# Streaming encoder step: first weights on ScalarE's queue, one query panel in the opening, later key transposes and operand splits

## The chip, the cores and the metric

The program runs on one core of a Trainium2 chip. The time is device microseconds of one execution. The kernel before took 2278.07 us, the median of three runs (2276.33 to 2283.46).

## The reference

One step of a one-layer encoder works on 1024 new prompt frames and on 8 running streams of 16 frames, with model width 2048 and 8 heads of 128 for each of two head groups. All of it is float32.

```
h = rms_norm(x, norm_pre);  p = h @ w_in            # 2048 -> 8 x 1024: q,k,v,gate of both groups
o_sb = stick_breaking(q_sb, k_sb, v_sb)             # samples also over 1024 cached frames
o_r  = retention(rope(q_r), rope(k_r), v_r, state)  # per-head decay, chunks of 64
y = concat(head_norm(o_sb)*silu(gate_sb), head_norm(o_r)*silu(gate_r)) @ w_out
x + rms_norm(y, norm_post)     # and the new keys, values and states
```

## The kernel before

**Products.** Each float32 operand is split into a high and a low float32r half (ScalarE copies `wh<-wr`, VectorE subtracts `wl<-wr,wh`; lines 167 and 168), and each product is three matmuls: high by high, low by high, high by low. Tokens are in two groups: group 0 holds prompt tiles 0 to 3 and the samples (640 columns, in pieces of 256 and 384), group 1 prompt tiles 4 to 7 (512 columns). A *panel* is one head's 128 columns of one of the eight projections, `project(g, mov, col(c, h))`: c is 0 for the stick-breaking queries, 1 keys, 3 gate, 4 retention queries, 5 retention keys, 7 retention gate. A panel of group 0 is 16 x 3 x 2 = 96 matmuls, one of group 1 is 48. The weights of a panel come in four loads `wr` of 256 KB on SP's queue, through five buffers.

**Stages.** The *opening* (lines 511 to 614) makes the panels q and k of retention head 0 while x arrives, computes row sums of squares (`squares`, on ScalarE, from loads `xt`), turns them into reciprocal roots (`rows_of`, VectorE) and spreads these over the partitions with four small matmuls `pb<-dg,ones` (`spread`, line 557). Then come the eight heads of group 0, the eight heads of group 1, and the *output stage*, in which seven products in the manner of Strassen are formed of sums of blocks. Its left operands are loaded and split by `left` and `left_sample` (tiles `ah`/`al` from loads `yr`, `sh`/`sl` from loads `ys`, `mh`/`ml` from loads `mr`).

**What sets the order.** A head's other work is written as generators, wrapped in `Job`. After each step of a panel, `tick()` advances one clock and runs the next step of at most one job that is due; what a generator yields is the number of ticks to its next step. So the constants `D_...` set the place of that work among the products. `drain(job)` calls `tick()` until the job is done, without products in between. A scheduler then orders each engine's instructions by their place in the program and by when it thinks that their inputs are ready; `pin` adds that an instruction may not stand ahead of the last product written before it, and `tied` adds the same in group 0 alone (`phase[0] == 0`). On the chip every engine, and SP's queue too, goes through its list in order.

**Jobs that the change touches.** `ret_branch` (lines 1022 to 1040) does the retention of one head: it writes the rotated keys to memory (`s_rk`), loads them back with blocks exchanged (`ro<-s_rk`, on SP), waits `D_TI` ticks, transposes them on VectorE (`rkn<-ro`, line 1032) and scales them (line 1036) before TensorE's `pS<-rv,rkn` (line 946). `retention` also reads the samples' state (`st<-state`, TensorE `pa<-st,rq`, line 976). In the first head of group 0 it starts in `ret_start`. The stick-breaking job of a head ends, for the samples, with the decode: `kp<-be` is transposed, `pd<-vn,kp` and `pd<-vc,kp` (lines 878 and 886) multiply the cached values `vc` (512 KB loads on SP, line 849, six buffers, so each waits until TensorE has read an older one), and `do<-pd` is copied, normed (`sq`, `or`, `do<-do,or`) and written (`s_o<-do`, on ScalarE's queue).

Of the kernel before, what the change touches and what calls it, by code (L numbers as in the profile page):

```python
# [18 lines left out]
P = 128  # L19
# [7 lines left out]
NT = PT + 1  # L27
SAMPLE = PT
WQ = 4
D_X = (5, 4)  # L30
X_PIECES = ((0, 256), (256, 384), (640, 512))
KC_AHEAD = 2
COLS = (0, 1, 3, 4, 5, 7)
# [55 lines left out]
def tile_hybrid_step(  # L89
# [151 lines left out]
    def drain(job):  # L241
        while job is not None and not job.done:
            tick()
# [67 lines left out]
    def left(gi, n, hi, lo, bufs, tag, deep):  # L311
        src = LEFT[n]
        raw = []

        def load(h):
            r = bufs.tile([P, 256], F32, name=tag, tag=tag, bufs=deep)
            if src[0] == "y":
                pin(nc.sync.dma_start(r, s_y[gi][src[1] * H + h][:, src[2] * 256 : src[2] * 256 + 256]))
            else:
                pin(nc.sync.dma_start(r, s_s[gi][h][:, src[1], :]))  # L320
            raw.append(r)

        for h in range(deep - 1):
            load(h)
        yield D_OP
        for h in range(HT):
            if h + deep - 1 < HT:
                load(h + deep - 1)
            r = raw.pop(0)
            pin(*split(hi[h], lo[h], r))  # L330
            yield D_OP

    def left_sample(kk, hi, lo, bufs, tag, deep):
        raw = []

        def load(h):
            r = bufs.tile([P, P], F32, name=tag, tag=tag, bufs=deep)
            pin(nc.sync.dma_start(r, s_y[0][kk * H + h][:, 4 * P : 5 * P]))
            raw.append(r)

        for h in range(deep - 1):
            load(h)
        yield D_OP
        for h in range(HT):
            if h + deep - 1 < HT:
                load(h + deep - 1)
            pin(*split(hi[h], lo[h], raw.pop(0)))
            yield D_OP
# [20 lines left out]
        made = [pool.tile([P, HT, n], F32R, name=t, tag=t, **kw) for t in tags]  # L369
        return [[t[:, h] for h in range(HT)] for t in made]  # L370

    def load_w(col):
        hs, ls = [], []
        for w in range(KT // WQ):
            wr = wp.tile([P, WQ, P], F32, name="wr", tag="wr", bufs=5)
            nc.sync.dma_start(wr, w_cols[COLS.index(col[0]), col[1], :, w * WQ : (w + 1) * WQ, :])
            wh = wp.tile([P, WQ, P], F32R, name="wh", tag="wh")
            wl = wp.tile([P, WQ, P], F32R, name="wl", tag="wl")
            split(wh, wl, wr)
            yield w, wh, wl  # L380
# [20 lines left out]
    def project(g, mov, col):  # L401
        acc = acc_banks(g)
        for w, wh, wl in load_w(col):
            products(mov, acc, g["pieces"], w, wh, wl)
        return list(zip(acc, g["pieces"]))
# [57 lines left out]
    with ExitStack() as s1:  # L463
# [47 lines left out]
        with tc.tile_pool(name="p0", bufs=2) as p0, tc.tile_pool(name="p0s", bufs=1) as p0s, tc.tile_pool(  # L511
            name="p0p", bufs=4, space=PSUM
        ) as p0p:
            warm = p0s.tile([P, 1], F32, name="warm")
            nc.scalar.activation(warm, eps, AF.Sqrt)
            ones = p0s.tile([P, P], F32, name="ones")
            nc.vector.memset(ones, 1.0)
            nc.sync.dma_start(pre, pre_cols)
# [1 line left out]
            def load_cols(piece, k, m):  # L520
                o, n = X_PIECES[piece]
                xc = p0.tile([P, m, n], F32, name=f"xc{piece}", tag=f"xc{piece}", bufs=4)
                src = x_cols[:, KT * o : KT * (o + n)].rearrange("p (k n) -> p k n", k=KT)
                nc.sync.dma_start(xc, src[:, k : k + m, :])
                return xc

            def squares(tiles, ssq, pace):
                todo = [(i, t, c) for i, t in enumerate(tiles) for c in range(2)]
                raw = []

                def load(i, t, c):
                    xt = p0.tile([P, HALF], F32, name="xt", tag="xc0", bufs=4)
                    nc.sync.dma_start(xt, x_rows(t)[:, c * HALF : (c + 1) * HALF])
                    raw.append(xt)

                for item in todo[:4]:
                    load(*item)
                yield pace
                for n, (i, t, c) in enumerate(todo):
                    xt = raw.pop(0)  # L540
                    pin(nc.scalar.activation(xt, xt, AF.Square, accum_out=ssq[:, c, i : i + 1]))
                    if n + 4 < len(todo):
                        load(*todo[n + 4])
                    yield pace
# [14 lines left out]

            def second_panel(w):  # L560
                wr = wp.tile([P, WQ, P], F32, name="wr", tag="wr", bufs=5)
                nc.sync.dma_start(wr, w_cols[COLS.index(5), 0, :, w * WQ : (w + 1) * WQ, :])
                wh, wl = (p0s.tile([P, WQ, P], F32R, name=f"w{s}5{w}") for s in "hl")
                split(wh, wl, wr)
                return w, wh, wl

            tiles = g0["tiles"]
            accs = [acc_banks(g0), acc_banks(g0)]
            first_panel = load_w(col(4, 0))
            panels = [], []  # L570
            xcs = [], []
            for w in range(KT // WQ):
# [31 lines left out]

            ret_values(g0, mov, 0, None, roots_first)
            rooted_tables((*first, *ropes), X_PIECES[:2])
            job = Job(squares(GROUPS[1]["tiles"], ssq[1], D_X[1]))
            tick()
            first = *first, pair["r"][:, :, 0, :], dict(rg=gate(project(g0, mov, col(7, 0)), "rg"))
            drain(job)  # L610
            nc.vector.tensor_copy(root_of[:, len(tiles) :], rows_of(ssq[1], "p4"))
            rb = p0s.tile([P, NB_TOK], F32, name="rb4")
            spread(rb, root_of, len(tiles), last)
            nc.scalar.dma_start(s_root, rb)

        kq = s1.enter_context(tc.tile_pool(name="kq", bufs=1))
        zp = s1.enter_context(tc.tile_pool(name="zp", bufs=1))
# [404 lines left out]
        def ret_branch(gi, g, h, rq, rk, rv, rest):  # L1022
            nt = len(g["tiles"])
            rkn = ep.tile([P, 6, P], F32, name="rkn", tag="rkn")

            out = Out(nt, "ro")
            s = turn_out(rk[:, : nt * P].rearrange("p (k t) -> p k t", t=P), f"s_rk{gi}_{h}")
            yield D_TO[phase[0]]
            raw = out.o.rearrange("p k d -> p (k d)")
            turn_in(s, raw, nc.sync)  # L1030
            yield D_TI[phase[0]]
            tied(nc.vector.transpose(rkn.rearrange("p k d -> p (k d)")[:, : nt * P], raw))
            if SAMPLE in g["tiles"]:
                nc.vector.tensor_scalar(rkn[:, 5, :], rkn[:, 4, :], dec[:, h, 5:6], None, ALU.mult)
                nc.vector.tensor_scalar(rkn[:, 4, :], rkn[:, 4, :], dec[:, h, 4:5], None, ALU.mult)
            nc.vector.tensor_scalar(rkn[:, :4, :], rkn[:, :4, :], dec[:, h, 1:2], None, ALU.mult)
            yield from retention(gi, g, h, out, rq, rk, rkn, rv)
            while "rg" not in rest:
                yield 3
            yield from out.finish(1, h, rest["rg"], rk, s_y[gi][H + h])  # L1040
# [35 lines left out]
        for gi, g in enumerate(GROUPS):  # L1076
# [7 lines left out]
            for h in range(H):  # L1084
# [29 lines left out]

                def attention():
                    nonlocal sb_job, sub, ip
                    acc = project(g, mov, col(0, h))
                    held = project(g, mov, col(1, h)) if h == H - 1 else None
                    drain(sb_job)
                    if gi == 1 and h == 0:  # L1120
# [459 lines left out]
```

## Time and profile before

| what | value |
|---|---|
| time, median of 3 runs | 2278.07 us |
| the profiled execution's own time | 2280.05 us |
| its span | 2278.3 us |
| PE busy | 2241.5 us (98%) |
| DVE, ACT, POOL busy | 1263.7, 919.8, 340.6 us (55%, 40%, 15%) |
| mean granted clock of TensorE | 0.996 |
| moved by DMA | 463.13 MB, mean 203 GB/s |

How to read it: the execution took 1.75 us more than its span, and the span is what the trace shows. TensorE is busy in nearly all of it, so what a change of order can move is the idle time of TensorE and the matmuls that run slower just after such a pause. In the timeline the first column is the start, the second the time until the instruction's end; matmuls overlap, so the pace of matmuls is the distance of their starts, not their duration. A timeline row stands for several instructions when it ends in x and a count.

### The profile page before, as it was taken

To read this page: it belongs to the slowest core of one execution; us is meant where nothing else is said; L and a number is where in the kernel's file an instruction comes from. 1 tells how busy PE (TensorE), PEld (TensorE's weight loads), DVE (VectorE), ACT (ScalarE), POOL (GpSimd) and SP (SyncE) were. 2 spreads that over 40 slices of the span, in tenths; PEclk is the share of its full clock that TensorE was granted. 3 is DMA by queue.
4 is the path that set the end of the run, shared out by engine and by line. 5 is a ranking of instruction groups with operands and counts; after the bars stand their busy time and mean duration, and the time that the engine had idled before them with its cause. 6 is when DMAs were issued, how large, how long until landed. Compare 5 with 4: busy or idle time off the path is not lost.

```text
span 2278.3 us, 38962 instructions
## 1 busy us (share of the span) xinstructions
PE 2241.5 (98%) x14306; PEld 2023.3 (89%) x14306; DVE 1263.7 (55%) x2606; ACT 919.8 (40%) x1951; POOL 340.6 (15%) x577
## 2 busy tenths in 40 slices
PE   8999999999999999999999999999999999999998
PEld 8999999999999999999887989888888988788886
DVE  5435544454545454456556665766665667555567
ACT  6433333333333333335343334343343445435363
POOL 0012120301202030121111111120212212000020
PEclk9999999999999999999999999999999999999999
DMA  8747656675656657578778888878787758865596
GB/s 284 233 153 199 196 159 194 176 220 159 182 194 181 194 165 209 177 200 269 193 225 207 220 220 235 206 226 238 220 231 213 216 165 190 252 205 182 146 222 172
DMA packets 440832, 463.13 MB, mean 203 GB/s; under 512 B 182336, under 2 KB 302144, under 8 KB 440128
## 3 DMA queue, kind: packets, MB, share of 16 engines
q1 hardware_dynamic: 318400, 300.16, 46.5%
q0 software_dynamic: 28720, 78.41, 12.3%
q10 hardware_dynamic: 93520, 82.07, 11.4%
q8 instruction: 112, 1.84, 0.3%
q14 instruction: 80, 0.66, 0.1%
HBM read 359.58 MB, written 110.36 MB: 206 GB/s over the span
## 4 chain that ended last, share of the span: by engine, by line
PE 88%; DMA 5%; DVE 3%; issue 2%; ACT 2%; SPq 0%; POOL 0%; DVEq 0%; ACTq 0%; POOLq 0%
PE acc L387 46%; PE accn L446 17%; PE a L1213 5%; PE a L1214 5%; PE a L1210 5%; PE pa L783 3%; PE z L753 2%; PE pd L886 1%; PE zc L822 1%; DMA ro<-s_rk 1%; DMA s_rk<-rk 1%; PE pa L931 1%; PE pS L946 1%; DVE kp L682 1%; DMA wr<-w_cols 1%
## 5 line engine op out<-in xcount | busy, mean ns | idle before, releaser
L387 PE MATMUL acc<-mh,wh 128*128 128x256 f32 (+2 forms) x2304 | 667.4, 341 | 6.9 <-ACT wh L167 6.9
L387 PE MATMUL acc<-ml,wh 128*128 128x256 f32 (+2 forms) x2304 | 662.7, 340 | 0.2
L387 PE MATMUL acc<-mh,wl 128*128 128x256 f32 (+2 forms) x2304 | 659.8, 338 | 0.0
L168 DVE TENSOR_TENSOR wl<-wr,wh 128x512 fp32r<-128x512 f32 x504 | 345.9, 689 | 428.0 <-ACT wh L167 401.7
L167 ACT ACTIVATE wh<-wr 128x512 fp32r<-128x512 f32 x504 | 317.3, 631 | 641.2 <-PE acc L387 347.2
L387 PEld LDWEIGHTS acc<-mh,wh 128*128 128x128 f32 x2304 | 421.4, 189 | 39.2 <-ACT wh L167 6.9
L387 PEld LDWEIGHTS acc<-ml,wh 128*128 128x128 f32 x2304 | 422.9, 189 | 32.1 <-issue 3.3
L387 PEld LDWEIGHTS acc<-mh,wl 128*128 128x128 f32 x2304 | 425.5, 189 | 27.8 <-DVE wl L168 0.2
L446 PE MATMUL accn<-whn,mh 128*128 128x256 f32 x1152 | 328.1, 285 | 0.0
L446 PE MATMUL accn<-wln,mh 128*128 128x256 f32 x1152 | 325.8, 283 | 0.8 <-DVE wln L168 0.8
L446 PE MATMUL accn<-whn,ml 128*128 128x256 f32 x1152 | 325.7, 283 | 0.0
L446 PEld LDWEIGHTS accn<-whn,mh 128*128 128x128 f32 x1152 | 220.7, 192 | 2.7 <-issue 0.8
L446 PEld LDWEIGHTS accn<-wln,mh 128*128 128x128 f32 x1152 | 220.7, 192 | 1.8 <-DVE wln L168 1.0
L446 PEld LDWEIGHTS accn<-whn,ml 128*128 128x128 f32 x1152 | 220.7, 192 | 0.0
L167 ACT ACTIVATE whn<-wrn 128x512 fp32r<-128x512 f32 x128 | 80.5, 632 | 183.2 <-PE acc L387 74.2
L168 DVE TENSOR_TENSOR wln<-wrn,whn 128x512 fp32r<-128x512 f32 x128 | 87.6, 687 | 117.4 <-ACT whn L167 113.5
L646 POOL DMA_DIRECT2D be<-s_be x128 | 94.1, 741 | 149.5 <-DMA s_be<-be 126.4
L682 DVE TENSOR_TENSOR_SCAN kp<-kp 128x1152 f32<-128x1152 f32 (+4 forms) x40 | 82.7, 2067 | 45.7 <-POOL kp L671 29.1
L809 POOL DMA_DIRECT2D kcT<-cache_k x64 | 34.6, 545 | 442.2 <-PE pd L886 268.2
L1210 PE MATMUL a<-wh,mh 128*128 128x512 f32 x240 | 94.0, 392 | 1.8 <-ACT wh L167 1.8
L671 POOL TENSOR_SCALAR_AFFINE_SELECT kb<-kb 128x128 f32<-128x128 f32 x64 | 29.8, 474 | 433.2 <-ACT kb L665 430.9
L1213 PE MATMUL a<-wl,mh 128*128 128x512 f32 x240 | 94.3, 393 | 0.2 <-DVE wl L168 0.2
(272 smaller groups left out, 2968.7 us busy)
## 6 DMA issues: line engine op xcount, KB each, us to landing
wr<-w_cols SPq DMA_DIRECT2D x384, 256.0 KB, 4.4
wrn<-w_rows SPq DMA_DIRECT2D x128, 256.0 KB, 3.7
kcT<-cache_k POOLq DMA_DIRECT2D x64, 512.0 KB, 8.2
vc<-cache_v SPq DMA_DIRECT2D x64, 512.0 KB, 6.0
wr<-s_b SPq DMA_DIRECT2D x80, 256.0 KB, 4.1
br<-w_out SPq DMA_DIRECT2D x64, 256.0 KB, 4.9
s_b<-br ACTq DMA_DIRECT2D x32, 512.0 KB, 5.5
wr<-w_out SPq DMA_DIRECT2D x48, 256.0 KB, 3.7
```

What stands on the lines that cost most here:

```text
L167: nc.scalar.activation(hi, src, AF.Copy),
L168: nc.vector.tensor_tensor(lo, src, hi.bitcast(F32), ALU.subtract),
L387: last = nc.tensor.matmul(a[:, :m], lhs[:, j, :], rhs[w][:, j, o : o + m], start=(w == 0 and j == 0 and n == 0), stop=(w == KT // WQ - 1 a ...
L446: anchor[0] = nc.tensor.matmul(a, lhs[q][:, jj, ts], rhs[:, j, :], start=(w == 0 and j == 0 and n == 0 and t % 2 == 0), stop=(w == KT // 2 ...
L646: q.dma_start(raw[32 * i : 32 * i + 32, :].rearrange("p (k a) -> p k a", a=32), s[:, :, 32 * i : 32 * i + 32].rearrange("k (j b) a -> b (k ...
L682: nc.vector.tensor_tensor_scan(rev, rev, rev, 1.0, ALU.mult, ALU.bypass)
L753: nc.tensor.matmul(z[:, :c], q2[a][:, i * P : (i + 1) * P], k2[b][:, s : s + c], start=(m == 0), stop=(m == 2),)
L783: nc.tensor.matmul(po[:, :P], at[:, j, :], vn[:, j, :], start=(j == 0), stop=(j == t))
L809: ready.append((kc, nc.gpsimd.dma_start(kc, cache_k[h, m // 4, m % 4])))
L1210: ins = nc.tensor.matmul(a, hi[k][:, ts], wh, start=first, stop=False)
L1213: nc.tensor.matmul(a, hi[k][:, ts], wl, start=False, stop=False)
L1214: anchor[0] = nc.tensor.matmul(a, lo[k][:, ts], wh, start=False, stop=last)
```

## The change

Four edits, built into one program:

1. *Opening loads.* The first `wr` of both first panels are issued on ScalarE's queue, ahead of the table load and the warming activation, which move behind them. The first 512 KB load of x becomes four of 128 KB.
2. *First query panel.* The second group's roots become part of the job (`later_roots`), with the pace of its squares changed from 4 to 5 ticks, and the panel `project(g0, mov, col(0, 0))` is written ahead of `drain(job)`; the first attention uses that panel. `ret_start` thereby stands one panel (48 ticks) later in the program.
3. *Key transposes.* `D_RK = (32, 19)` takes the place of `D_TI = (32, 13)` in `ret_branch`: nothing changes in group 0, six ticks more in group 1.
4. *Operand splits.* `left` and `left_sample` wait `D_LAND` = 12 ticks after their first loads, not `D_OP` = 2.

```diff
--- before.py
+++ after.py
@@ -27,7 +27,9 @@
 NT = PT + 1
 SAMPLE = PT
 WQ = 4
-D_X = (5, 4)
+D_X = (5, 5)
+D_RK = (32, 19)
+D_LAND = 12
 X_PIECES = ((0, 256), (256, 384), (640, 512))
 KC_AHEAD = 2
 COLS = (0, 1, 3, 4, 5, 7)
@@ -322,7 +324,7 @@
 
         for h in range(deep - 1):
             load(h)
-        yield D_OP
+        yield D_LAND
         for h in range(HT):
             if h + deep - 1 < HT:
                 load(h + deep - 1)
@@ -340,7 +342,7 @@
 
         for h in range(deep - 1):
             load(h)
-        yield D_OP
+        yield D_LAND
         for h in range(HT):
             if h + deep - 1 < HT:
                 load(h + deep - 1)
@@ -369,11 +371,10 @@
         made = [pool.tile([P, HT, n], F32R, name=t, tag=t, **kw) for t in tags]
         return [[t[:, h] for h in range(HT)] for t in made]
 
-    def load_w(col):
-        hs, ls = [], []
+    def load_w(col, first=nc.sync):
         for w in range(KT // WQ):
             wr = wp.tile([P, WQ, P], F32, name="wr", tag="wr", bufs=5)
-            nc.sync.dma_start(wr, w_cols[COLS.index(col[0]), col[1], :, w * WQ : (w + 1) * WQ, :])
+            (nc.sync if w else first).dma_start(wr, w_cols[COLS.index(col[0]), col[1], :, w * WQ : (w + 1) * WQ, :])
             wh = wp.tile([P, WQ, P], F32R, name="wh", tag="wh")
             wl = wp.tile([P, WQ, P], F32R, name="wl", tag="wl")
             split(wh, wl, wr)
@@ -511,8 +512,6 @@
         with tc.tile_pool(name="p0", bufs=2) as p0, tc.tile_pool(name="p0s", bufs=1) as p0s, tc.tile_pool(
             name="p0p", bufs=4, space=PSUM
         ) as p0p:
-            warm = p0s.tile([P, 1], F32, name="warm")
-            nc.scalar.activation(warm, eps, AF.Sqrt)
             ones = p0s.tile([P, P], F32, name="ones")
             nc.vector.memset(ones, 1.0)
             nc.sync.dma_start(pre, pre_cols)
@@ -521,7 +520,9 @@
                 o, n = X_PIECES[piece]
                 xc = p0.tile([P, m, n], F32, name=f"xc{piece}", tag=f"xc{piece}", bufs=4)
                 src = x_cols[:, KT * o : KT * (o + n)].rearrange("p (k n) -> p k n", k=KT)
-                nc.sync.dma_start(xc, src[:, k : k + m, :])
+                step = 1 if piece == k == 0 else m
+                for j in range(0, m, step):
+                    nc.sync.dma_start(xc[:, j : j + step, :], src[:, k + j : k + j + step, :])
                 return xc
 
             def squares(tiles, ssq, pace):
@@ -559,14 +560,17 @@
 
             def second_panel(w):
                 wr = wp.tile([P, WQ, P], F32, name="wr", tag="wr", bufs=5)
-                nc.sync.dma_start(wr, w_cols[COLS.index(5), 0, :, w * WQ : (w + 1) * WQ, :])
+                (nc.sync if w else nc.scalar).dma_start(wr, w_cols[COLS.index(5), 0, :, w * WQ : (w + 1) * WQ, :])
+                if w == 0:
+                    warm = p0s.tile([P, 1], F32, name="warm")
+                    nc.scalar.activation(warm, eps, AF.Sqrt)
                 wh, wl = (p0s.tile([P, WQ, P], F32R, name=f"w{s}5{w}") for s in "hl")
                 split(wh, wl, wr)
                 return w, wh, wl
 
             tiles = g0["tiles"]
             accs = [acc_banks(g0), acc_banks(g0)]
-            first_panel = load_w(col(4, 0))
+            first_panel = load_w(col(4, 0), nc.scalar)
             panels = [], []
             xcs = [], []
             for w in range(KT // WQ):
@@ -604,14 +608,21 @@
 
             ret_values(g0, mov, 0, None, roots_first)
             rooted_tables((*first, *ropes), X_PIECES[:2])
-            job = Job(squares(GROUPS[1]["tiles"], ssq[1], D_X[1]))
+            def later_roots():
+                yield from squares(GROUPS[1]["tiles"], ssq[1], D_X[1])
+                rstd = rows_of(ssq[1], "p4")
+                nc.vector.tensor_copy(root_of[:, len(tiles) :], rstd)
+                yield 6
+                rb = p0s.tile([P, NB_TOK], F32, name="rb4")
+                spread(rb, root_of, len(tiles), last)
+                yield 4
+                nc.scalar.dma_start(s_root, rb)
+
+            job = Job(later_roots())
             tick()
             first = *first, pair["r"][:, :, 0, :], dict(rg=gate(project(g0, mov, col(7, 0)), "rg"))
+            queries = project(g0, mov, col(0, 0))
             drain(job)
-            nc.vector.tensor_copy(root_of[:, len(tiles) :], rows_of(ssq[1], "p4"))
-            rb = p0s.tile([P, NB_TOK], F32, name="rb4")
-            spread(rb, root_of, len(tiles), last)
-            nc.scalar.dma_start(s_root, rb)
 
         kq = s1.enter_context(tc.tile_pool(name="kq", bufs=1))
         zp = s1.enter_context(tc.tile_pool(name="zp", bufs=1))
@@ -1028,7 +1039,7 @@
             yield D_TO[phase[0]]
             raw = out.o.rearrange("p k d -> p (k d)")
             turn_in(s, raw, nc.sync)
-            yield D_TI[phase[0]]
+            yield D_RK[phase[0]]
             tied(nc.vector.transpose(rkn.rearrange("p k d -> p (k d)")[:, : nt * P], raw))
             if SAMPLE in g["tiles"]:
                 nc.vector.tensor_scalar(rkn[:, 5, :], rkn[:, 4, :], dec[:, h, 5:6], None, ALU.mult)
@@ -1114,7 +1125,7 @@
 
                 def attention():
                     nonlocal sb_job, sub, ip
-                    acc = project(g, mov, col(0, h))
+                    acc = project(g, mov, col(0, h)) if gi or h else queries
                     held = project(g, mov, col(1, h)) if h == H - 1 else None
                     drain(sb_job)
                     if gi == 1 and h == 0:
```

Three places at which the order moves. First, TensorE at the second group's roots. `acc` are the products of the first query panel's two pieces, `pb` the spreading of the roots. Before:

```order
L387 MATMUL acc_932<-mh_182,wl 128x384
L387 MATMUL acc_1134<-mh_176,wh 128x256
L557 MATMUL pb<-dg,ones 128x128 x2
L387 MATMUL acc_1135<-mh_176,wh 128x384
L387 MATMUL acc_1134<-ml_177,wh 128x256
L387 MATMUL acc_1135<-ml_177,wh 128x384
L387 MATMUL acc_1134<-mh_176,wl 128x256
L387 MATMUL acc_1135<-mh_176,wl 128x384
L557 MATMUL pb<-dg,ones 128x128 x2
L387 MATMUL acc_1134<-mh_176,wh 128x256
```

After:

```order
L388 MATMUL acc_1093<-ml_177,wh 128x256
L388 MATMUL acc_1094<-ml_177,wh 128x384
L388 MATMUL acc_1093<-mh_176,wl 128x256
L388 MATMUL acc_1094<-mh_176,wl 128x384
L388 MATMUL acc_1093<-mh_176,wh 128x256
L558 MATMUL pb<-dg,ones 128x128 x2
L388 MATMUL acc_1094<-mh_176,wh 128x384
L558 MATMUL pb<-dg,ones 128x128
L388 MATMUL acc_1093<-ml_177,wh 128x256
L388 MATMUL acc_1094<-ml_177,wh 128x384
L558 MATMUL pb<-dg,ones 128x128
L388 MATMUL acc_1093<-mh_176,wl 128x256
```

The first spreading moved from behind the panel's first matmul to behind its thirteenth, twelve matmuls later.

Second, SP's queue in head 1 of group 0, around the decode of head 0: `wr` are weights, `vc` cached values, `ro`, `so` and `be` come back from memory after exchange. Before:

```order
L849 DMA vc<-cache_v 128x1024
L376 DMA wr<-w_cols 128x512 x3
L849 DMA vc<-cache_v 128x1024
L376 DMA wr<-w_cols 128x512
L646 DMA be<-s_bd_2211 32x36x32 x4
L849 DMA vc<-cache_v 128x1024 x2
L376 DMA wr<-w_cols 128x512 x2
L849 DMA vc<-cache_v 128x1024 x2
L376 DMA wr<-w_cols 128x512 x2
L646 DMA ro<-s_rk_1_2444 32x20x32 x4
L646 DMA so<-s_o_0_4_0_2526 32x16x32 x4
L908 DMA dT<-c_dt 128x256
```

After:

```order
L377 DMA wr<-w_cols 128x512 x5
L860 DMA vc<-cache_v 128x1024
L657 DMA ro<-s_o_0_5_0_2085 32x20x32 x4
L860 DMA vc<-cache_v 128x1024
L657 DMA be<-s_bd_2199 32x36x32 x4
L860 DMA vc<-cache_v 128x1024 x2
L657 DMA so<-s_o_0_4_0_2443 32x16x32
L860 DMA vc<-cache_v 128x1024 x2
L657 DMA so<-s_o_0_4_0_2443 32x16x32 x3
L377 DMA wr<-w_cols 128x512 x7
L657 DMA ro<-s_rk_1_2493 32x20x32 x4
L377 DMA wr<-w_cols 128x512 x3
```

Before, two `wr` stood ahead of the last two `vc` of head 0 and two behind them; now all `vc` and `so` stand in a block behind `be`, and the `wr` that were among them follow the block, seven in a row. The first of the seven is the fourth quarter of the gate panel of head 1. ScalarE has, at the same place (`do` is the decode's output), before:

```order
L167 ACTIVATE wh<-wr 128x512
L703 ACTIVATE sq,ssq_1292<-do 128x128
L183 ACT_TABLE_LOAD
L183 ACTIVATE or<-ov 128x1
L167 ACTIVATE wh<-wr 128x512
L639 DMA s_o_0_1_0_2700<-do 128x128
L167 ACTIVATE wh<-wr 128x512
```

After:

```order
L650 DMA s_rk_1_2493<-rk 128x5x128
L714 ACTIVATE sq,ssq_1286<-do 128x128
L185 ACTIVATE or<-ov 128x1
L650 DMA s_o_0_1_0_2626<-do 128x128
L169 ACTIVATE wh<-wr 128x512 x5
L481 ACT_TABLE_LOAD
```

The copy `wh<-wr` of that quarter stands behind `sq<-do`, `or<-ov` and the store `s_o<-do`, and on TensorE the second half of the decode (16 rows `pd<-vc,kp`) stands ahead of the matmuls of that quarter. The two halves of the decode are ten matmuls of the panel apart now, and were 74 apart before. TensorE after:

```order
L388 MATMUL acc_2466<-mh_180,wl 128x256
L388 MATMUL acc_2467<-mh_180,wl 128x384
L897 MATMUL pd<-vc,kp 32x256 x8
L924 MATMUL rs<-rq,rk 128x128
L897 MATMUL pd<-vc,kp 32x256 x4
L924 MATMUL rs<-rq,rk 128x128
L897 MATMUL pd<-vc,kp 32x256 x4
L388 MATMUL acc_2466<-mh_182,wh 128x256
L388 MATMUL acc_2467<-mh_182,wh 128x384
```

Third, ScalarE at the entry of the output stage, before:

```order
L167 ACTIVATE wh_21377<-wr_21375 128x512
L167 ACTIVATE ah<-yr 128x256 x3
L167 ACTIVATE wh_21396<-wr_21394 128x512
L167 ACTIVATE sh<-ys 128x128
L167 ACTIVATE ah<-yr 128x256
L167 ACTIVATE sh<-ys 128x128
L167 ACTIVATE wh_21421<-wr_21419 128x512
L167 ACTIVATE sh<-ys 128x128 x3
L167 ACTIVATE ah<-yr 128x256
L167 ACTIVATE wh_21467<-wr_21465 128x512
L167 ACTIVATE sh<-ys 128x128 x3
```

After:

```order
L169 ACTIVATE wh_21380<-wr_21378 128x512
L731 DMA s_y_7_161<-sg 128x512
L169 ACTIVATE ah<-yr 128x256 x3
L169 ACTIVATE wh_21399<-wr_21397 128x512
L169 ACTIVATE ah<-yr 128x256
L169 ACTIVATE wh_21424<-wr_21422 128x512
L169 ACTIVATE sh<-ys 128x128 x3
L169 ACTIVATE ah<-yr 128x256
L169 ACTIVATE wh_21458<-wr_21456 128x512
L169 ACTIVATE sh<-ys 128x128 x3
L169 ACTIVATE ah<-yr 128x256
```

The third copy of the weights (`wh_21421` before, `wh_21424` after) stood behind two `sh<-ys`, and now stands ahead of the first of them.

VectorE's list keeps the order of `rkn<-ro`, `kp<-be` and `so<-pa` in each head of group 1; in the first head in which they stand close together it is, before:

```order
L1032 STREAM_TRANSPOSE rkn<-ro 128x512
L743 STREAM_TRANSPOSE kp<-be 128x1024
L1036 TENSOR_SCALAR rkn<-rkn,dec 128x512
L168 TENSOR_TENSOR wl<-wr,wh 128x512
L786 COPY so<-pa 128x128
```

After:

```order
L1043 STREAM_TRANSPOSE rkn<-ro 128x512
L754 STREAM_TRANSPOSE kp<-be 128x1024
L1047 TENSOR_SCALAR rkn<-rkn,dec 128x512
L170 TENSOR_TENSOR wl<-wr,wh 128x512
L797 COPY so<-pa 128x128
```

Nothing moved among these five.

## The prediction

> **What bounds the kernel now.** I read the busy times of the page, then TensorE's waits, then the timeline at each wait of 1 us or more.
>
> ```profile
> span 2278.3 us, 38962 instructions
> PE 2241.5 (98%) x14306; PEld 2023.3 (89%) x14306; DVE 1263.7 (55%) x2606; ACT 919.8 (40%) x1951; POOL 340.6 (15%) x577
> ...
> PE pa L783 <- DVE kp L743: 8.1, 7, 2.4
> ```
>
> TensorE is idle for 2278.3 - 2241.5 = 36.8 us. None of the edits takes a matmul away, so a gain can only come out of these 36.8 us and out of the slow matmuls behind a pause; a loss has no such limit. The execution took 2280.05 us, 1.98 us above the median of 2278.07. I sum changes against 2280.05 and take 1.98 off at the end. A run can tell about 0.3%, 6.8 us, from no change.
>
> **Opening.** Six rows carry it.
>
> ```profile
> 6.87 0.58 PE L387 MATMUL acc<-mh,wh 128*128 128x256 f32 x1 [6.87 <-ACT wh L167]
> 10.10 0.58 PE L387 MATMUL acc<-ml,wh 128*128 128x256 f32 x1
> 13.16 0.28 PE L387 MATMUL acc<-ml,wh 128*128 128x256 f32 x1
> 8.29 0.63 ACT L167 ACTIVATE wh<-wr 128x512 fp32r<-128x512 f32 x1 [1.07 <-DMA wr<-w_cols]
> 10.92 0.63 ACT L167 ACTIVATE wh<-wr 128x512 fp32r<-128x512 f32 x1 [0.47 <-DMA wr<-w_cols]
> 11.88 0.63 ACT L167 ACTIVATE wh<-wr 128x512 fp32r<-128x512 f32 x1
> ```
>
> TensorE starts at 6.87 and runs without gaps from 10.10, because the second panel's weights come at 8.29. With both first weights on a queue of their own, and x in quarters, the start can come some 1.5 us sooner. But the second quarter of the weights is ready at 11.88 + 0.63 = 12.51, and TensorE reaches it at about 13.16: only 0.65 us of the lead survives, since as many bytes are ahead of that quarter as before. I take 0.5; if the quarter also comes later the loss is about 1, and if it comes sooner the gain is 1.5.
>
> Here the Trainium skill, "DMA: Bandwidth & Descriptors", section "Issuing engines are not separate DMA queues", says that issuing from several engines saves only the sequencer's time to start a transfer. That would make this term smaller still; no row of before has weights on ScalarE's queue, so it is untested here, and the sum would change by 0.5 at most.
>
> **First query panel.** The wait for the roots:
>
> ```profile
> 87.74 1.15 PE L557 MATMUL pb<-dg,ones 128*128 128x128 f32 x4 [3.12 <-DVE dg L555]
> 88.54 0.67 PE L387 MATMUL acc<-mh,wh 128*128 128x384 f32 x1
> 91.38 0.45 PE L387 MATMUL acc<-ml,wh 128*128 128x256 f32 x2
> 91.67 0.46 PE L387 MATMUL acc<-mh,wl 128*128 128x256 f32 x2
> 85.06 0.16 DVE L547 TENSOR_TENSOR ssq<-ssq 128x4 f32<-128x4 f32 x1 [0.35 <-ACT xt L541]
> 87.40 0.48 DVE L555 TENSOR_SCALAR dg<-ident,root_of 128x128 f32<-128x128 f32 x2
> 87.80 0.88 DVE L468 TENSOR_TENSOR rg<-acc,roots 128x256 f32<-128x256 f32 x2
> ```
>
> Two panel matmuls take 91.67 - 91.38 = 0.29 us, one 0.147. From 88.54 to 91.38 stand seven of them and four pb, about 1.03 + 0.3 us of work in 2.84: 1.5 us of slow clock behind the pause. All told it costs 3.12 + 1.5 = 4.6. The panel's matmuls stood there already, all but one behind pb; twelve now come ahead, 12 x 0.147 = 1.8 us later. VectorE's chain is 2.34 from sum to first dg, and in the new order the two gate rows rg, which took 0.88 behind the first dg, are ahead of it. So the wait falls by 1.8 - 0.9 = 0.9; I take 1.0, with a little of the slow clock. Nothing at all is the low end, all 4.6 the high end.
>
> The retention of head 0 starts 48 ticks later. Its wait for the state has a price too:
>
> ```profile
> 152.68 1.44 PE L976 MATMUL pa<-st,rq 128*32 128x256 f32 x6 [0.86 <-DMA st<-state]
> ```
>
> The loads now stand behind fewer 512 KB loads, so I count 1.0 (0 to 1.2).
>
> **The new wait in head 1.** In the order after, the fourth quarter of the gate panel is copied (wh) behind the decode of head 0, and TensorE needs that copy right behind the decode. These rows of before price the same steps:
>
> ```profile
> 209.10 1.05 PE L783 MATMUL pa<-vn,kb 128*128 128x128 f32 x8
> ...
> 213.86 0.46 PE L878 MATMUL pd<-vn,kp 128*128 128x128 f32 x2
> 214.25 1.93 PE L886 MATMUL pd<-vc,kp 128*32 128x256 f32 x32
> 216.12 0.56 PE L387 MATMUL acc<-mh,wh 128*128 128x256 f32 x2
> 214.95 0.80 SPq L849 DMA_DIRECT2D vc<-cache_v  x2
> 215.91 0.40 ACTq L639 DMA_DIRECT2D s_o<-so  x1
> 229.17 0.29 DVE L894 COPY do<-pd 128x128 f32<-128x128 f32 x1 [2.00 <-PE pd L886]
> 230.69 1.28 ACT L183 ACT_TABLE_LOAD   x1
> 232.74 0.69 DVE L168 TENSOR_TENSOR wl<-wr,wh 128x512 fp32r<-128x512 f32 x1
> 234.24 0.34 ACTq L639 DMA_DIRECT2D s_o<-do  x1
> ```
>
> And these, of vc and of s_o over the whole trace, then of the one s_o<-so between 200 and 236 us, say how long such transfers take from issue to landing:
>
> ```profile
> DMA to landing us min/median/max: 3.7/6.0/11.0
> DMA to landing us min/median/max: 1.6/3.5/10.4
> ...
> s_o<-so ACTq DMA_DIRECT2D x1, 256.0 KB, 10.4
> ```
>
> Let the first half of the decode start at t. It takes 216.12 - 213.86 = 2.26; ten panel matmuls take 1.47; the second half 1.87; two rs some 0.4 (my estimate). Without waits TensorE is at the fourth quarter at t + 6.0. But the last two vc need buffers that the first half frees: the vc row of before starts 214.95 - 213.86 = 1.1 behind t, the second of the pair 0.4 later. With 6.0 to land they are there at t + 7.5, and pd ends at t + 8.3. From do to the store took 234.24 - 229.17 = 5.07, of which 1.28 was a table load that the new order doesn't have there, and some 0.6 the wl in the middle of the chain, which now stands behind it: 3.2. With the issue of the store (0.34) and the copy of the weights (0.63, as in the opening) it is t + 12.4. TensorE idles 12.4 - 6.0 = **6.4 us**, and the slow clock behind it costs 1.5 more, as at the roots: 7.9. With the shortest landing of vc, 3.7, the loss is 5.6; with SP held up it is more, below. Nothing else hides it: ScalarE and VectorE go through their lists in order, and the other products stand behind the quarter.
>
> **Later key transposes.** The longest of the waits behind kp:
>
> ```profile
> 1242.54 0.71 DVE L1032 STREAM_TRANSPOSE rkn<-ro 128x512 f32<-128x512 f32 x1 [2.35 <-DMA ro<-s_rk]
> 1243.17 1.20 DVE L743 STREAM_TRANSPOSE kp<-be 128x1024 f32<-128x1024 f32 x1
> ...
> 1244.43 3.31 PE L783 MATMUL pa<-vn,kp 128*128 128x128 f32 x16 [2.44 <-DVE kp L743]
> ```
>
> VectorE stands still for ro and kp is behind it. Six ticks are 6 x 0.23 = 1.4 us, and would let kp go first. But `tied` orders nothing in group 1, so six ticks only lower the transpose's priority, and VectorE's list after has rkn ahead of kp still. The loads of ro are not moved. So this 2.44 stays, and the term is what small shifts give: 0.5, between -2 (pS, just behind rkn, waits longer) and +3.7 (the 2.44 with its slow matmuls, 3.31 where 2.05 is usual, gone).
>
> **Later operand splits.** The entry of the output stage:
>
> ```profile
> 1963.20 0.31 ACT L167 ACTIVATE sh<-ys 128x128 fp32r<-128x128 f32 x1 [6.49 <-DMA ys<-s_y]
> ...
> 1963.92 0.61 ACT L167 ACTIVATE wh<-wr 128x512 fp32r<-128x512 f32 x1
> ...
> 1964.59 0.49 PE L1210 MATMUL a<-wh,mh 128*128 128x512 f32 x1 [1.80 <-ACT wh L167]
> ...
> 1964.00:1969.00 5.00, 4.18 (x11) 3.11 (x12) 4.17 (x12) 2.38 (x8) 0.00 (x0) 0.66 0.66 189
> 1975.00:1980.00 5.00, 5.00 (x24) 4.14 (x23) 3.67 (x8) 3.47 (x8) 0.00 (x0) 1.00 0.90 342
> ```
>
> ScalarE waited for ys in front of a weight copy. In the new order that copy is ahead of sh, so the 1.80 goes. Behind it the clock is 0.66 (column PEclk, the third from the right), and 11 matmuls take the time in which 5.00/24 x 11 = 2.3 of 4.18 busy us would do: 1.9 more. Together 3.7. What is late next is the following sh, which now has a copy behind it as well; I take **3.0** (1 to 3.7).
>
> "TensorE: Matmul & The Clock Gate" of the Trainium skill, section "Why this matters for your kernels", advises against idle gaps of more than about 3 us, since a window of idleness halves the clock. By that a pause of 1.8 would cost no clock and this term would be 1.8, and the sum 1.2 worse. The clock of 0.66 behind 1.80 us speaks against that here.
>
> **Sum.** Gains 0.5 + 1.0 + 1.0 + 0.5 + 3.0 = 6.0, loss 7.9: 1.9 us more, 2280.05 + 1.9 = 2281.95, and less 1.98 about **2280**. No change that can be told.
>
> **Rivals.** *The edits at the roots and of the keys give all they can:* the roots come before TensorE does (4.6), kp goes first (3.7), the splits give 3.7, opening and state 1.5 and 1.2: 14.7 against a loss in head 1 of 5.6. 2278.07 - 9.1 = 2269. Against it speaks the order, in which rkn is still ahead of kp and dg has more ahead of it; for it, that both waits are just short of what the edits shift. Without kp it is 2273. *SP is held up in head 1, slower:* ahead of the last two vc stands so, which needs the store s_o<-so to have landed. In before that store came 215.91 - 209.10 = 6.8 us behind the start of the last pa, and in the new order 88 panel matmuls (12.9 us) and that pa's 1 us lie ahead of t: it is issued near t - 7.1. Landing in up to 8.2 us it is there by t + 1.1 and delays nothing; each us beyond delays vc, do and the weights. At 10.4, its longest, that is 2.2, and with the longest landing of vc, 11.0, another 5.0: the wait is 13.6, the loss 15.1, and with gains of 6.0 the time is 2278.07 + 9.1 = 2287. The medians of 3.5 and 6.0 speak against it; that the longest landing of s_o is the one at this very place of before speaks for it. *The change doesn't do what it says:* the panel in the opening delays nothing because its matmuls stood there before; then neither head 1 nor the roots move, and splits and opening alone give 2274.5. The rows of the order after speak against it.
>
> **How the numbers follow.** Gains and the new wait nearly cancel: 0.5, 2280, by itself 2274 to 2286. The gains in full: 0.22, 2269. SP held up: 0.2, 2287. No effect in head 1 and at the roots: 0.08, 2274.5. Faster by over 0.3% (below 2271.3) takes nearly all of the second case and a little of the last, 0.22. Slower by over 0.3% (above 2284.9) takes half of the third, a tenth of the first, and 0.09 for a further wait of this kind in the reordered stretch between 90 and 205 us, of which I priced only the state: 0.24. The other 0.54 lies between. The range, 2268 to 2290, reaches to both rivals.
>
> **What would show it.** The wait of acc for wh in head 1, near 210 us, of 4 to 8, with SP's vc rows just ahead; if it is not there, my largest term is wrong and the time is near 2272. The wait of pb should be near 2, that of st gone; 2.44 at kp should stand; 1.80 at the first a of the output stage should be gone, with the clock at 1.00. If head 1 shows more than 10 us, SP was held up.

## The result, and the profile after

The changed kernel takes 2293.64 us (median of 6 runs) against 2278.41 us of the kernel before, measured beside it (6 runs): 1.0069 of the time before, 95% interval 1.0054 to 1.0085, some 15 us slower. The forecast was 2280, the range 2268 to 2290; the time lies above both. First the head of the page of the changed kernel, then TensorE's waits:

```profile
span 2292.5 us, 38978 instructions
PE 2239.7 (98%) x14306; PEld 2020.0 (88%) x14306; DVE 1264.0 (55%) x2606; ACT 913.5 (40%) x1947; POOL 343.5 (15%) x577
```

```profile
PE pa L794 <- DVE kp L754: 12.3, 8, 3.0
PE acc L388 <- ACT wh L169: 10.9, 1, 10.9
PE acc L388 <- ACT mh L174: 7.9, 1, 7.9
...
PE a L1221 <- ACT ah L169: 1.5, 1, 1.5
...
PE pb L558 <- DVE dg L556: 1.1, 1, 1.1
```

The reader is to see that TensorE's busy time is the same within 2 us (2241.5 before) and its idle time is 2292.5 - 2239.7 = 52.8 us, where it was 36.8. The 16 us are waits. The wait of acc for wh is the one that the prediction named; the start waits for mh now, not for wh; the waits for kp grew from 8.1 to 12.3. The pauses themselves in TensorE's timeline, in order of time:

```profile
7.91 0.80 PE L388 MATMUL acc<-mh,wh 128*128 128x256 f32 x2 [7.91 <-ACT mh L174]
87.89 0.71 PE L558 MATMUL pb<-dg,ones 128*128 128x128 f32 x4 [1.09 <-DVE dg L556]
228.57 0.90 PE L388 MATMUL acc<-mh,wh 128*128 128x256 f32 x2 [10.89 <-ACT wh L169]
1254.58 2.05 PE L794 MATMUL pa<-vn,kp 128*128 128x128 f32 x16 [2.69 <-DVE kp L754]
1912.55 0.49 PE L942 MATMUL pa<-rv,sc 128*128 128x128 f32 x2 [0.64 <-DVE sc L926]
1918.17 1.60 PE L794 MATMUL pa<-vn,kp 128*128 128x128 f32 x12 [1.49 <-DVE ro L951]
1921.79 0.49 PE L942 MATMUL pa<-rv,sc 128*128 128x128 f32 x2 [1.32 <-DVE so L797]
1933.77 1.83 PE L794 MATMUL pa<-vn,kp 128*128 128x128 f32 x14 [3.05 <-DVE kp L754]
1972.18 0.50 PE L1221 MATMUL a<-wh,ah 128*128 128x512 f32 x1 [1.45 <-ACT ah L169]
```

Two places make the loss. In head 1 of group 0 stand 10.89 us. In the last head of group 1, between 1912 and 1934, stand 0.64 + 1.49 + 1.32 + 3.05 = 6.5 us, where before had this one pause of 0.95:

```profile
1901.72 0.49 PE L946 MATMUL pS<-rv,rkn 128*128 128x128 f32 x2 [0.95 <-DVE rkn L1036]
```

The wait of 2.69 at 1254 is the 2.44 of before, which was to stay. The wait for the state is gone.

**Head 1, step by step.** The rows of the changed kernel that answer to those priced in the prediction, from the timelines of five engines, with the sum of the key loads kcT of this stretch (issue times from first to last), then TensorE's clock in the pause and behind it (the third number from the right):

```profile
209.91 0.38 PE L889 MATMUL pd<-vn,kp 128*128 128x128 f32 x2
210.93 0.81 SPq L860 DMA_DIRECT2D vc<-cache_v  x2
211.78 3.27 SPq L657 DMA_DIRECT2D so<-s_o  x3
215.09 15.24 SPq L377 DMA_DIRECT2D wr<-w_cols  x7
212.07 1.13 POOL L820 DMA_DIRECT2D kcT<-cache_k  x2 [27.66 <-PE pd L897]
L820 POOL DMA_DIRECT2D kcT<-cache_k x6: 528/532/577, 212.1 to 218.0; - x6
217.75 0.29 DVE L905 COPY do<-pd 128x128 f32<-128x128 f32 x1 [10.79 <-PE pd L897]
221.00 0.34 ACTq L650 DMA_DIRECT2D s_o<-do  x1
227.89 2.69 ACT L169 ACTIVATE wh<-wr 128x512 fp32r<-128x512 f32 x4 [8.22 <-DMA wr<-w_cols]
```

```profile
218.00:228.00 10.00, 0.00 (x0) 0.00 (x0) 2.00 (x11) 0.71 (x4) 0.53 (x1) 0.55 1.07 345
229.00:232.00 3.00, 3.00 (x13) 3.00 (x13) 2.27 (x4) 1.51 (x3) 0.00 (x0) 0.50 0.41 124
```

With t = 209.91: the last vc are issued at t + 1.0 (prediction 1.1), do is copied at t + 7.8 (8.3), the store is issued at t + 11.1 (11.5). So far the chain is as priced. But ScalarE, free at 221.34, does not get its weights: it waits for the transfer of wr until 227.89. The DMA engines are busy throughout (share 1.07 in the second last column, 345 GB/s). The first wr stands in SP's queue behind vc and so, and the two halves of the decode, ten matmuls apart, have freed the buffers for six loads kcT of 512 KB on GpSimd's queue, all issued between 212.1 and 218.0. Before, two of these started near 216 and four from 228 on.

The three so, 64 KB each in small pieces, are what is slow in SP's queue. Their rows of the stretch from 205 to 232 us:

```profile
L657 SPq DMA_DIRECT2D so<-s_o x3: 480/552/2139, 211.8 to 214.5; - x3
DMA to landing us min/median/max: 11.9/12.9/13.2
```

The last of them lands at 214.5 + 12.9 = 227.4, and the first wr half a microsecond later. Behind the pause the clock is 0.50 for three microseconds, in which 13 matmuls run; at the prediction's pace of 0.147 they would take 1.9 us. That is most of the 1.5 us that were forecast for it.

**The last head.** VectorE, ScalarE and SP of the changed kernel just ahead of the pause of 3.05, and then VectorE's rows at the same transpose before:

```profile
1931.61 0.42 DVE L170 TENSOR_TENSOR ml<-mr,mh 128x256 fp32r<-128x256 f32 x1 [3.06 <-ACT mh L169]
1932.61 1.11 DVE L754 STREAM_TRANSPOSE kp<-be 128x896 f32<-128x896 f32 x1
1931.17 0.42 ACT L169 ACTIVATE mh<-mr 128x256 fp32r<-128x256 f32 x1 [3.02 <-DMA mr<-s_s]
1924.24 8.14 SPq L322 DMA_DIRECT2D mr<-s_s  x4
```

```profile
1910.28 0.75 DVE L168 TENSOR_TENSOR ml<-mr,mh 128x256 fp32r<-128x256 f32 x2
...
1912.35 1.10 DVE L743 STREAM_TRANSPOSE kp<-be 128x896 f32<-128x896 f32 x1
```

The transpose kp<-be, for which TensorE waits, stands behind splits ml of the first output product; these wait for ScalarE's mh, and that for the loads mr, whose issue takes SP until 1932. Before, two of these splits (ml of 128x256) stood ahead of kp in VectorE's timeline; now there are six.

### The profile page after: what moved, and what is told of

Read it like the earlier page. It is cut to its first block, busy times and chain, and to the rows that moved or that the text cites. A ratio compares the mean times of both kernels' runs of the same rounds, so it can differ in the third digit from the quotient of the medians.

```text
span 2292.5 us, 38978 instructions
## 1 busy us (share of the span) xinstructions
PE 2239.7 (98%) x14306; PEld 2020.0 (88%) x14306; DVE 1264.0 (55%) x2606; ACT 913.5 (40%) x1947; POOL 343.5 (15%) x577
## 3 DMA queue, kind: packets, MB, share of 16 engines
q10 hardware_dynamic: 93808, 82.59, 11.5%
```

## The experiments

The comparison in each is with the kernel before on the same chip (medians 2277.18 us for e1 to e4, 2277.70 for e5 to e8 and 2278.01 for e9 to e12). 0.1% is 2.3 us; microseconds given with a ratio are worked out from the ratio, and differences of medians depart from them by up to 1.5 us.

**e1_open: edit 1 alone.** The edit is the part of the diff in load_w, load_cols and second_panel.

> Only the opening loads of edit 1. The changed kernel started TensorE at 7.91 us (before 6.87) but was 0.42 late at 40 us. If the edits add up, this one alone gives +0.4 us, within 0.05% of before, with the first product again near 7.9. If the later start is only made up because edit 2 follows, it gives +1.

1.0006 (0.9997 to 1.0014). The first product is late here too:

```profile
8.01 0.79 PE L386 MATMUL acc<-mh,wh 128*128 128x256 f32 x2 [8.01 <-ACT mh L172]
```

Edit 1 is worth nothing that can be told. The interval, -0.7 to +3.2 us, holds both expectations and the forecast gain of 0.5 as well; what the trace shows is a later start.

**e2_query: edit 2 alone.** The part with later_roots, queries and D_X.

> Only the first query panel and the job of later roots. Theory: the retention of head 0 starts 48 ticks later, is unfinished at head 1's retention queries, and draining it advances the decode too by ticks without products; so the wait of acc for wh near 215 us (10.9 in the changed kernel) is here alone, and with the gain at the roots (about 3.5) the time is +7 to +9 us. Rival: the wait needs the other edits' order as well; then it is absent or under 3 us here and the time is -3 to 0.

1.0047 (1.0035 to 1.0059), +10.7 us, with the wait in head 1:

```profile
229.28 0.90 PE L387 MATMUL acc<-mh,wh 128*128 128x256 f32 x2 [11.65 <-ACT wh L167]
```

The wait is edit 2's own, and the cost is above the +7 to +9 expected. The gain at the roots was put too high: see below.

**e3_keys: edit 3 alone.** D_RK for D_TI in ret_branch.

> Only the six ticks on the key transposes of group 1. Theory: the changed kernel's waits in the last head of group 1 (sc 0.64, ro 1.49, so 1.32, kp 3.05; 0.95 at pS before) come from this edit, in whose drain of the last but one head 8 ticks become 3 and the next 5 become 6; then it is +4 to +6 us here with those waits. Rival: they come from edit 2's shift of the jobs or from edit 4; then this run is within 1 us of before.

1.0042 (1.0029 to 1.0054), +9.6 us (6.6 to 12.3), more than the +4 to +6 expected, and the four waits of the last head are here, while group 0 is as before:

```profile
1902.32 0.49 PE L932 MATMUL pa<-rv,sc 128*128 128x128 f32 x2 [0.76 <-DVE sc L916]
1908.17 1.60 PE L784 MATMUL pa<-vn,kp 128*128 128x128 f32 x12 [1.68 <-DVE ro L941]
1911.65 0.49 PE L932 MATMUL pa<-rv,sc 128*128 128x128 f32 x2 [1.17 <-DVE so L787]
1923.44 2.15 PE L784 MATMUL pa<-vn,kp 128*128 128x128 f32 x14 [2.87 <-DVE kp L744]
```

They are 6.5 us where before had 0.95, and behind the last of them the clock was 0.68 from 1923 to 1928 us, which I estimate at 1.6 us (0.32 of 5). That is about 7 of the 9.6; the rest isn't placed.

**e4_land: edit 4 alone.** D_LAND in left and left_sample.

> Only the ten ticks on the operand splits. The prediction had 3.0 us of gain from the copy of the weights being ahead of sh. The changed kernel has 1.45 of wait for ah at the entry instead of 1.80 for wh, so by that this run gives -0.5 to -2 us. If the splits cost more later in the output stage, it is above 0.

0.9997 (0.9988 to 1.0005): no difference. TensorE's pause at the entry of the output stage and, with it, VectorE's row of that copy:

```profile
1967.68 0.50 PE L1214 MATMUL a<-wl,mh 128*128 128x512 f32 x1 [2.02 <-DVE wl L169]
```

```profile
1965.27 0.89 DVE L305 TENSOR_TENSOR br<-br 128x256 f32<-128x256 f32 x2 [2.07 <-DMA br<-s_y]
1966.07 0.28 DVE L169 TENSOR_TENSOR sl<-ys,sh 128x128 fp32r<-128x128 f32 x1
...
1966.94 0.69 DVE L169 TENSOR_TENSOR wl<-wr,wh 128x512 fp32r<-128x512 f32 x1
```

The high half of the weights comes in time now; the low half stands behind br and sl on VectorE, and br waits 2.07 for a load of its own (br<-s_y). The wait of 1.80 for wh became one of 2.02 for wl.

**e5_nodrain: edit 2 without the drain.**

The change stands at each of the five places where the retention gives such a number of ticks; one is shown.

```diff
-            yield D_RET[phase[0]]        # and 2 * D_RET[phase[0]]
+            yield (6 if phase[0] == h == 0 else D_RET[phase[0]])
```

> Edit 2 alone, with the retention of head 0 paced by 6 ticks, not 9, so that it is done before head 1's retention queries and nothing is drained there. Theory: the 26 ticks without products are the whole cost; the wait of acc for wh in head 1 (11.65 us in edit 2 alone) is gone and the time is within 2 us of before. Rival: the later start of the retention costs by itself; then it stays 5 us or more above before.

0.9989 (0.9981 to 0.9998): 2.5 us faster than before, a little more than expected, and 13 us faster than e2_query. TensorE's pauses between 41 and 300 us are these:

```profile
87.36 0.71 PE L557 MATMUL pb<-dg,ones 128*128 128x128 f32 x4 [1.18 <-DVE dg L555]
233.48 0.49 PE L938 MATMUL pa<-rv,sc 128*128 128x128 f32 x2 [1.77 <-DVE sc L922]
```

The panel in the opening costs nothing. What costs is that the retention of head 0, registered 48 ticks later, is drained for 26 ticks (counted in the program; none here) at head 1's retention queries, and that a drain runs every job that is due, the decode of head 0 among them. The decode's halves come together, and the loads behind them.

**e6_nokeys: edit 2 without head 1's cached keys.** This kernel leaves out the cached keys of head 1.

```diff
-                ready.append((kc, nc.gpsimd.dma_start(kc, cache_k[h, m // 4, m % 4])))
+                if h == 1:
+                    ready.append((kc, nc.gpsimd.memset(kc, 0.0)))
+                else:
+                    ready.append((kc, nc.gpsimd.dma_start(kc, cache_k[h, m // 4, m % 4])))
```

> Edit 2 alone, with the cached keys of head 1 left out: their loads (eight of 512 KB, kcT on GpSimd's queue) are memsets to zero, with the order of all engines as in edit 2 alone. In edit 2 alone ScalarE is free for the weights at 221.3 us and they land only near 228. Theory: they share the DMA engines with six of the key loads, 3 MB; without these they land before about 222.5, the wait falls from 11.65 to 5 or 6, near the 6.4 of the prediction, and the time is 5 to 7 us below edit 2 alone. Rival: they wait behind vc and the small pieces of so in SP's own queue; then they land as late, the wait stays at 10 or more and the time at 2287.

1.0020 (1.0011 to 1.0029), 6.2 us below e2_query by the ratios and 3.8 by the medians. TensorE's pause, and then ScalarE's copies and SP's issues in it:

```profile
221.64 0.90 PE L387 MATMUL acc<-mh,wh 128*128 128x256 f32 x2 [4.38 <-ACT wh L167]
```

```profile
220.96 2.19 ACT L167 ACTIVATE wh<-wr 128x512 fp32r<-128x512 f32 x4 [1.71 <-DVE do L714]
213.79 9.48 SPq L376 DMA_DIRECT2D wr<-w_cols  x7
```

The copy starts right behind the store, released by do and no longer by a transfer. So the wait of 11.65 is 4.4 us of the decode's chain and 7.3 us of weights that land late because of the key loads; SP's queue with its so in front is the same in both. The time of the three so without the key loads:

```profile
DMA to landing us min/median/max: 4.8/4.9/5.5
```

In e2_query it is 13.6 in the median. In both kernels, as in the changed one, the first wr lands 0.5 us behind the last so (218.5 behind 218.0 here, 228.6 behind 228.1 in e2_query). So the theory and its rival are each right in part: the key loads are the cause, and the late weights stand behind so in SP's own queue, which the key loads stretch. How late the weights would be without so ahead of them no run shows. The Trainium skill says in "DMA: Bandwidth & Descriptors", section "Issuing engines are not separate DMA queues", that transfers of all issuing engines run on the same 16 DMA engines and interleave; the 7.3 us that go with loads of another queue agree.

**e7_keys04 and e8_keys4: edit 3 by heads.** The two differ in the condition alone:

```diff
-            yield D_TI[phase[0]]
+            yield D_RK[phase[0]] if h < 4 else 13 if phase[0] else 32      # e8_keys4: h == 4
```

> Edit 3 in heads 0 to 3 of group 1 alone. Counted in the program, the drains ahead of heads 6 and 7 stay at 8 and 5 ticks as before. Theory: the cost of edit 3 comes from head 4's later job, by which these drains become 3 and 6; so this run has none of the waits of the last head (sc, ro, so, kp) and is within 1.5 us of before. Rival: each head's transpose costs a share; then it is +3 to +5.

1.0003 (0.9995 to 1.0012), with none of the four waits.

> Edit 3 in head 4 of group 1 alone; the drains become 3 and 6 ticks. Theory: the full cost of edit 3, +8 to +10 us, with the four waits in the last head (about 6.5 us together), though its own transpose is not moved. Rival: the last heads' own later transposes cause these waits; then none of them is here and the time is within 1.5 us of before.

1.0016 (1.0007 to 1.0024), +3.6 us: slower, but less than half of edit 3. Of the four waits the longest is here:

```profile
1917.56 2.13 PE L784 MATMUL pa<-vn,kp 128*128 128x128 f32 x14 [3.73 <-DVE kp L744]
```

So a six-tick delay in head 4 makes a wait in head 7, whose own job is not delayed. The drains in heads 5 and 6 (3 and 6 ticks, where e7_keys04 has the 8 and 5 of before) are the likely way, though head 4's own work moves too. It does not make all of edit 3.

**e10_keysno4: edit 3 in all heads but 4** (h != 4 as the condition).

> Edit 3 in all heads of group 1 but head 4. The drains are 8 and 5 ticks as before. Theory: without the changed drains the transpose kp<-be of the last head keeps its place among the operand splits and the time is within 1.5 us of before. Rival: the later transposes of heads 5 to 7 cost by themselves the part that head 4 alone (+0.16%) left of edit 3's +0.42%; then it is +4 to +6 us.

1.0011 (1.0003 to 1.0020), +2.5 us (0.7 to 4.6), between the two expectations. The wait at the same matmuls of the last head is there, though the drains are as before:

```profile
1917.24 1.80 PE L784 MATMUL pa<-vn,kp 128*128 128x128 f32 x14 [2.78 <-DVE or L185]
```

The theory that the drains are the cause of edit 3's loss falls as the only cause: the later jobs of heads 5 to 7 bring the same wait without them. What the runs have in common is the order on VectorE at the last head's kp<-be:

| kernels | splits ml ahead of kp | wait of the 14 matmuls behind kp |
|---|---|---|
| before, e1, e2, e4, e5, e7, e9, e11 | 2 | none |
| e12_fast | 2 | 0.51 us |
| e8_keys4, e10_keysno4 | 4 | 3.73, 2.78 us |
| e3_keys, changed kernel | 6 | 2.87, 3.05 us |

In the last four kernels the last splits ahead of kp wait 2.75 to 3.46 us for ScalarE's mh, as in the rows of the changed kernel above; so this order is the cause of the long wait. With six splits ahead the other three waits of the last head come too. Head 4 alone (+0.16%) and the others alone (+0.11%) make less than all together (+0.42%), but the intervals are too wide to tell whether they add up, and why the order brings the other three waits is open.

**e9_no3: edits 1, 2 and 4.**

> The changed kernel without edit 3 (edits 1, 2 and 4). Theory: the parts add up, so it is at edit 2 alone, +9 to +11 us against before, and the last head of group 1 has none of the waits at sc, ro, so and kp. Rival: edits 1 and 4 give back some of it; then +5 to +8.

1.0046 (1.0034 to 1.0058), as edit 2 alone. In the last head there is the 0.95 of before and no more. Edit 3 adds the rest of the changed kernel's 1.0069, some 5 us, less than the 9.6 it costs alone: the four edits alone sum to 0.92%, and whether the difference is more than noise can't be told from these intervals.

**e11_fixed: all four edits, mended** (the pace of e5_nodrain, and h < 4 as the condition of edit 3).

> All four edits, with the retention of head 0 paced by 6 ticks and edit 3 in heads 0 to 3 only, so that no drain differs from before but one of a tick in the output stage. Theory: the sum of the parts measured alone, +0.06 -0.11 +0.03 -0.03%: within 2.5 us of before, and neither the wait in head 1 nor those of the last head. Rival: the edits cost together what they don't cost alone; then 5 us or more above before.

0.9994 (0.9984 to 1.0003): neither loss is there, and no difference from before can be told.

**e12_fast: edit 2 with the pace of 6, and edit 4.**

> Edit 2 with the retention of head 0 paced by 6 ticks, and edit 4: the two parts that were not slower alone. Expected -0.11 -0.03%: 2 to 4 us below before. If the faster run of edit 2 was chance, it is within 1 us.

0.9989 (0.9980 to 0.9998), 2.5 us faster than before. It is not faster than edit 2 mended alone, so edit 4 adds nothing that can be told. This and e5_nodrain are the fastest versions, by about 0.1%.

## Why the prediction was wrong

The direction of the sum (slower by 1.9 us) held, its size did not. In part that was luck: a third or more of the loss comes from the key transposes, for which a gain was forecast. Step by step:

- **Head 1: mechanism right, size wrong.** The wait is at the place, of the instruction and from the drained decode that the order showed, and its chain ran as priced to t + 11.1. The step that failed is "With the issue of the store (0.34) and the copy of the weights (0.63 ...) it is t + 12.4": it takes the weights as landed. The copy started at t + 18.0. The wait was 10.89, not 6.4, and in edit 2 alone it falls from 11.65 to 4.4 without the key loads (e6_nokeys). So the priced part was 2 too long, mainly because TensorE came to the quarter at t + 7.5 there and not at t + 6.0, and the missing part is 7 us. The prediction looked at what the decode's buffers free on SP (vc) and not at what they free on GpSimd (kcT), nor at the three so ahead of the weights in SP's queue.
- **Later key transposes: wrong, the largest error.** Forecast a gain of 0.5, between -2 and +3.7; alone the edit costs 9.6 us. The step that failed is "six ticks only lower the transpose's priority, and VectorE's list after has rkn ahead of kp still". It is true of rkn, kp and so among themselves and says nothing on the operand splits, among which the last head's kp<-be stands: behind two of them before, behind six after. The rows of the list that stand ahead of the prediction are an earlier head's. Since a tick runs at most one job that is due, and a drain runs all of them, six ticks in one job also move others.
- **Later operand splits: no gain.** "In the new order that copy is ahead of sh, so the 1.80 goes" was true of ScalarE only. VectorE has the low half behind br, and 1.80 became 2.02 (e4_land). In the changed kernel 1.45 is left, for ah, and the clock behind it is 1.00, as forecast.
- **Roots: the wait fell, the gain was small.** 1.09 is below the "near 2" forecast, but the 3.12 of before was one execution. In e1_open it is

```profile
86.04 0.71 PE L556 MATMUL pb<-dg,ones 128*128 128x128 f32 x4 [1.80 <-DVE dg L554]
```

  and in the other five kernels without edit 2 it is 1.63 (e3_keys), 1.38 (e4_land), 1.69, 1.55 and 1.68 (e7, e8, e10). Against these the change gains 0.3 to 0.7; in the kernels with edit 2 the wait is 0.73 to 1.99.
- **Opening: no gain.** That "the start can come some 1.5 us sooner" failed: ScalarE copies both panels' weights ahead of x, and the second comes at 6.83, so that the first mh starts at 7.37 and TensorE at 7.91, a microsecond later than before.
- **State:** the wait of 0.86 is gone, as forecast.
- **The rival of SP held up** named the longer wait, and its sign (more than 10 us) came, but by other transfers: s_o<-so landed in 2.3 us and vc in 5.2 (median of the stage), so neither of its conditions came. What held the queue up were the three so behind vc.

In sum, by edit: edit 2 was forecast at 7.9 - 1.0 - 1.0 = +5.9 us and measured +10.7, edit 3 at -0.5 and measured +9.6 alone and some +5 beside the others, edit 4 at -3.0 and measured -0.7, edit 1 at -0.5 and measured +1.4. That is some 5 us missed in head 1, 5 to 10 at the key transposes and about 2 each at the splits and in the opening, where the intervals are as wide, all in one direction.

## What to carry to other kernels

Where jobs are advanced by a common clock, a later start of one is paid wherever something waits for its end: look up who drains it, and what else that drain moves. Price a reordered wait to its last input, the data's landing and what stands ahead of it in its queue included, and ask of every buffer that is freed sooner which transfers, on all queues, start sooner with it. A wait seen in one execution is not yet a gain: look what stands next on each engine that makes the data, and how long the same wait is in other executions.

## What the runs showed of the hardware that was not expected

Three loads of 64 KB in small pieces (32x16x32) took 11.9 to 13.2 us to land when six of 512 KB were started on another queue beside them, and 4.8 to 5.5 without those (e6_nokeys, the same queue otherwise). The 256 KB of weights right behind them took 12.8 us, where 4.4 is the median of such loads before.

The slow clock behind a pause does not go by its length. In the changed kernel 16 matmuls took 2.05 us behind a pause of 2.69 (the row at 1254 above); before, the same 16 took 3.31 behind 2.44. The granted clock in them was 1.00 and 0.58. At this place the other kernels have 2.77 to 3.41 us behind pauses of 2.31, 2.57 and 2.73 (e10, e12, e9), and 2.05 behind pauses of 2.62 to 3.48 (e1, e2, e3, e4, e6). The rule of the Trainium skill that the prediction weighed ("TensorE: Matmul & The Clock Gate", section "Why this matters for your kernels"), no gaps of more than about 3 us, is not borne out as a bound in either direction: in e1_open a pause of 3.48 at the same place left these 16 at 2.05:

```profile
1249.05 2.05 PE L785 MATMUL pa<-vn,kp 128*128 128x128 f32 x16 [3.48 <-DVE kp L745]
```
